# Low parts of split weights by a copy on ScalarE and an accumulating DMA, in a hybrid encoder block on one Trainium2 core

## The chip, the cores and the metric

The kernel runs on one core of one Trainium2 chip. The core has five engines that work at the same time, each through its own list of instructions and strictly in that list's order: TensorE (PE in the profile; its weight loads are shown apart, as PEld), VectorE (DVE), ScalarE (ACT), GpSimd (POOL) and SyncE (SP), which in this kernel only issues DMAs. Sixteen DMA engines move data between HBM and SBUF, and within SBUF. Engines wait for one another by semaphores. The metric is the device time of one execution in microseconds (us); less is better. The kernel before takes 2143.35 us, the median of three runs (2143.24 to 2143.78).

## The reference

One layer of an encoder on 1024 tokens of width 1024, in float32:

```python
h = rms_norm(x, g_mix)
glu_a, glu_b, q, k, v, z, a_in, b_in, gate_a, gate_b = split_cols(h @ w_in)
c = glu_a * sigmoid(glu_b)
c = silu(layer_norm(depthwise_conv(c, conv_dw_w) + conv_dw_b))       # 31 taps
y_conv = c @ w_conv_out
q, k, v = split_cols(silu(depthwise_conv([q, k, v], qkv_conv_w)))    # 5 taps
o = gated_delta_rule(q, k, v, ...) forward + the same backward       # 8 heads, chunks of 64
y_delta = (rms_norm(o) * silu(z)) @ w_delta_out
x = x + (sigmoid(gate_a) * y_conv + sigmoid(gate_b) * y_delta) @ w_o
gt, up = split_cols(rms_norm(x) @ w_gate_up)                         # 2 x 2816 columns
x = x + (silu(gt) * up) @ w_down
x = x + sigmoid(rms_norm(x) @ w_pl_gate) * rms_norm(p @ w_pl_proj)
return rms_norm(x, g_final)
```

Nearly all arithmetic is in the dense products with `w_in`, `w_conv_out`, `w_delta_out`, `w_o`, `w_gate_up`, `w_down` and `w_pl_gate`. All of them have the same form in the kernel, and the change is in how their weights are prepared.

## The kernel before, in words

**Split products.** TensorE reads the operands of a dense product as float32r, a form of float32 with fewer bits. To keep the precision, every operand is the sum of two such tiles, a high part `hi` and a low part `lo`, and a product is three matmuls (`mm3`): hi by hi, hi by lo of the activations, lo of the weights by hi. The first two need only `hi` of the weight tile; the third needs its `lo`. `split` makes the two parts from a float32 tile: ScalarE copies the tile into `hi`, which rounds it (`CAST` in the profile), and VectorE subtracts `hi` from the tile into `lo`.

**Weight tiles.** A weight tile is 512 rows by 128 columns, as four blocks of 128x128 side by side: 128 partitions by 512 values. SyncE loads it from HBM into a raw tile (four slots of tag `raw`, or one of the eight shared `mid` slots), `split` fills a tile of pool `wp` (tag `w`, `[P, 2, 4, P]`: both parts), and TensorE uses it as the stationary operand in 12 matmuls of 512 columns (four blocks, three matmuls each) or in 24, when both halves of the tokens follow one another. Pool `wp` has six slots (`N_W`), and tiles of a line are given out in the order of the program. `load_w` loads and splits; `split_w` splits a tile that is there already.

**Products of sums.** The delta projection (`seven`) and the gate and up products of the FFN (`gate_up`, `product`, `first_half`) use Winograd's form of Strassen's product: seven products in place of eight, of sums of the weights' quarters a11, a12, a21, a22. The sums are made by VectorE, some of them in place. In program order a block of `gate_up` uses the weights a11, s = a21 + a22, then s - a11 written over s, a11 - a21 written over a21, a12, then a12 - s written over a12, and a22. So two of the seven tiles are sources of a split, are overwritten by VectorE and are split again at once: s and a12. There are 22 column blocks: the first (`GU_PLAIN = 1`) is done by plain products, whose four weight tiles stay in their slots between the two halves of the tokens; of the next four (`GU_AHEAD = 4`) the products of a11 and a12 are done ahead, between those halves, while x is still being prepared; the other 17 go through whole.

**Stages.** In time: RMSNorm and transposes of x; the products with `w_in`, interleaved with the depthwise convolutions (336 instructions `big<-big,cw` on VectorE) and the delta rule of 8 heads, in chains of small matmuls with VectorE and ScalarE between them; LayerNorm and `w_conv_out`; then `w_delta_out` with the merge, `w_o`, the FFN, the per-layer embedding and the final norm. The delta rule and the convolutions end near 1100 us.

**What sets the order.** The block is written down as a list of instructions on stand-ins for tiles. `Plan.order` gives it an order by list scheduling: for each engine it takes, among the instructions whose inputs are there by its own clock, the most urgent one; durations, latencies and numbers of buffers are constants in the code (a 512-column float32r matmul is 512/2400 + 0.003 = 0.216 us in it). The order is fixed when the program is built; on the chip each engine only follows its list and waits. Weight splits have a more urgent level than the work they feed. Every operation is recorded by a helper, so one line of code stands for many instructions: L237 matmul, L242 transpose, L259 ScalarE copies and casts, L266 ScalarE activations, L282 VectorE, L310, L314 and L318 GpSimd (powers, memsets, selects), L330 SyncE's DMAs. In the profile, `w` is a weight tile, `raw` and `mid` its sources, `ps` a PSUM bank, `m` a tile of 512 columns in the delta rule's output step, `rn` its norm factors.

Of the kernel before, what the change touches and what calls it, by code (L numbers as in the profile page):

```python
# [36 lines left out]
class Buf:  # L37
    """A stand-in for a tile."""
# [15 lines left out]
class View:  # L54
    """Part of a tile: partitions [p0, p1), free dimensions as (stride, size) from an offset."""
# [40 lines left out]
    def fold(self, *sizes):  # L96
        """The last free dimension cut into dimensions of these sizes."""
        s, n = self.dims[-1]
        dims = []
        for k in reversed(sizes):  # L100
            dims.append((s, k))
            s *= k
        return View(self.buf, self.p0, self.p1, self.off, self.dims[:-1] + dims[::-1], self.cast)
# [4 lines left out]
    def spread(self, *shape):  # L108
        """Dimensions of size one repeated to these sizes."""
# [28 lines left out]
class Op:  # L138
    """An instruction: its engine, how to issue it, and what it reads and writes."""


# functions that need a table of their own in ScalarE, and the price of a change of tables
# [3 lines left out]
# a DMA: from its issue to its data, and bytes in a microsecond  # L146
DMA_LAT, DMA_RATE = 1.6, 300000.0
HOLD = {"dve": 0.24, "act": 0, "pe": 0}

# from the end of an instruction to the start of one that needs it, by the engines of both  # L150
# [7 lines left out]
class VPool:  # L158
# [5 lines left out]
    def tile(self, shape, dtype=F32, tag=None, bufs=None, line=None, cap=99, stream=None):  # L164
        """line: tiles of a line are given out in the order of the program, at most cap at a time."""
# [7 lines left out]
class Plan:  # L173
# [11 lines left out]
    # -- recording  # L185
    def add(self, eng, fn, outs, ins, cost, nbytes=0, table=None):
# [3 lines left out]
        o.idx = len(self.ops)  # L190
        o.key = (self.level, o.idx)
# [38 lines left out]
    # -- engines  # L230
    def matmul(self, out, lhsT, rhs, start, stop):
        n = rhs.n
        if rhs.buf.dtype == F32R and rhs.cast is None:
            cost = max(0.107, n / 2400 + 0.003)
        else:
            cost = 2 * max(0.107, n / 1200)
# [4 lines left out]
    def transpose(self, out, in_, ident):  # L241
        self.add("pe", lambda: self.nc.tensor.transpose(out.ap(), in_.ap(), ident.ap()), [out], [in_, ident], 0.107)  # L242
# [91 lines left out]
    # -- scheduling  # L334
    def order(self):
# [6 lines left out]
        free_slots = {}     # (pool, tag) -> times at which slots come free  # L342
        queue = {}          # line -> tiles in program order
# [8 lines left out]
        wait = {e: [] for e in engs}       # heap by ready time: dependencies all scheduled  # L352
        avail = {e: [] for e in engs}      # heap by key: ready at the engine's time
# [6 lines left out]
        held = []                            # of a later phase  # L360
        last_end = {}
        parked = {}                          # (pool, tag) -> ops that wait for a slot
# [10 lines left out]
        def slots_ready(o, now):  # L373
            """None when it can go now; else (time or None, (pool, tag))."""
# [20 lines left out]
        while len(done) < total:  # L395
# [43 lines left out]
            # worth the wait: something more urgent is about to be ready  # L439
# [24 lines left out]
            else:  # L464
                free[e] = o.end = now + o.cost
# [36 lines left out]
    # -- issue  # L502
# [54 lines left out]
# slots of each kind of tile, and what goes before what  # L557
# [11 lines left out]
YT_AFTER = (2, 1)  # L569
WO_LEAD = 6  # L570
# [9 lines left out]
# products of part 1 in order (k, q, v, g: glu, z, l: logits, p: per-layer embedding; with the head or  # L580
# block), and those that fill in
# [6 lines left out]
def ORDER(f):  # L588
    """The block up to the delta rule's end, in the order in which it is written down."""
# [1176 lines left out]
```

## Time and profile before

| | |
|---|---|
| runs before | 2143.78, 2143.35, 2143.24 us; median 2143.35 |
| span of the profiled execution | 2144.9 us, 1.5 us above the median of the runs |
| TensorE busy | 2094.7 us (98%), 10434 instructions |
| VectorE busy | 1606.4 us (75%) |
| ScalarE busy | 1089.8 us (51%) |
| GpSimd busy | 129.5 us (6%) |
| VectorE's low parts of weights, `w<-raw,w` and `w<-mid,w` | 340 + 125 instructions, 221.6 + 85.9 us |
| DMA | 278.69 MB, mean 130 GB/s |

How to read it. The profile is of one execution on the chip. Busy shares are averages over stages with different limits, so they are read by stage with the view that cuts the time into windows. The view of waits says for each engine how long it stood idle and what it waited for last. The chain is the work that ended last, followed back. A line of a group reads: line, engine, operation, output<-inputs by tile names, shapes, count | busy time, mean time of one in ns | idle time of the engine before it, and what ended it. A landing time of a DMA runs from its issue to its data.

### The profile page before, as it was taken

Reading aid. Unit: us, or ns where it says so; the run is one execution under the profiler, and the core shown is the slowest. Engines: PE = TensorE matmul, PEld = TensorE weight load, DVE = VectorE, ACT = ScalarE, POOL = GpSimd, SP = SyncE. Lnnn points to the kernel's source line nnn. Section 1 sums busy time; section 2 is a strip of 40 time slices with the busy share of each in tenths; the row PEclk is TensorE's granted clock in tenths of the full one; section 3 lists DMA queues with packets and bytes.
Section 4 is the critical chain, followed back from the end, with each engine's and each line's share of the span. In section 5 each row is a group of like instructions: output and inputs, shape, how many; then the busy total and the mean of one; then the engine's idle time right before and its main releaser. Section 6 shows DMA issues by size and latency. Waiting matters only on the chain.

```text
span 2144.9 us, 29696 instructions
## 1 busy us (share of the span) xinstructions
PE 2094.7 (98%) x10434; PEld 1736.6 (81%) x10434; DVE 1606.4 (75%) x2621; ACT 1089.8 (51%) x2501; POOL 129.5 (6%) x203
## 2 busy tenths in 40 slices
PE   7999999999999999999999999999999999999998
PEld 5888788878888788878888888888888888888888
DVE  4488999977898989887687868786666667452676
ACT  6636656756656655767775435533323334121542
POOL 1000201110100111011100000000000000000000
PEclk9999999999999999999999999999999999999999
DMA  6233224522423422635468687432222227231253
GB/s 213 100 123 127 84 81 138 187 79 79 138 89 120 146 74 79 197 122 182 157 213 254 195 262 229 123 99 84 80 78 84 84 80 273 67 95 39 66 170 108
DMA packets 289077, 278.69 MB, mean 130 GB/s; under 512 B 17209, under 2 KB 217074, under 8 KB 288928
## 3 DMA queue, kind: packets, MB, share of 16 engines
q1 hardware_dynamic: 288928, 276.79, 40.3%
q8 instruction: 82, 1.34, 0.3%
q14 instruction: 67, 0.55, 0.1%
HBM read 198.02 MB, written 78.71 MB: 129 GB/s over the span
## 4 chain that ended last, share of the span: by engine, by line
PE 86%; ACT 7%; DVE 5%; issue 1%; DMA 1%; SPq 0%; POOL 0%; DVEq 0%; POOLq 0%; ACTq 0%
PE ps L237 84%; ACT big L259 4%; DVE big L282 3%; PE ps L242 2%; DVE mid L282 1%; ACT big L266 1%; ACT m L266 1%; DVE w L282 1%; ACT w L259 1%; DMA big<-in_x_dram 1%; DMA d<-mid 0%; ACT mid L266 0%; SPq L330 0%; ACT L266 0%; ACT mid L259 0%
## 5 line engine op out<-in xcount | busy, mean ns | idle before, releaser
L237 PE MATMUL ps<-big,w 128*128 128x512 f32 (+1 forms) x7524 | 1848.7, 399 | 0.9 <-ACT w L259 0.8
L237 PEld LDWEIGHTS ps<-big,w 128*128 128x128 f32 x7524 | 1383.4, 189 | 305.3 <-ACT w L259 1.2
L282 DVE SCALAR_TENSOR_TENSOR big<-big,cw 128x1024 f32<-128x1024 f32 x336 | 434.2, 1299 | 17.3 <-ACT big L266 12.3
L259 ACT CAST w<-raw 128x512 fp32r<-128x512 f32 (+2 forms) x340 | 198.3, 589 | 365.0 <-PE ps L237 288.4
L282 DVE TENSOR_TENSOR w<-raw,w 128x512 fp32r<-128x512 f32 (+2 forms) x340 | 221.6, 659 | 124.9 <-ACT w L259 119.3
L282 DVE TENSOR_TENSOR big<-ps,big 128x512 f32<-128x512 f32 (+1 forms) x132 | 89.9, 687 | 86.4 <-PE ps L237 76.2
L259 ACT CAST w<-mid 128x512 fp32r<-128x512 f32 x125 | 77.2, 621 | 149.5 <-PE ps L237 109.5
L282 DVE TENSOR_TENSOR w<-mid,w 128x512 fp32r<-128x512 f32 x125 | 85.9, 688 | 62.3 <-ACT w L259 61.6
L237 PEld LDWEIGHTS ps<-big 128*128 128x128 f32 x784 | 101.9, 195 | 16.1 <-issue 9.1
L237 PE MATMUL ps<-big 128*128 128x128 f32 (+1 forms) x784 | 107.2, 283 | 7.7 <-ACT big L259 5.1
L282 DVE TENSOR_TENSOR big<-big 128x512 fp32r<-128x512 f32 (+2 forms) x159 | 107.0, 707 | 8.7 <-ACT big L259 8.4
L259 ACT COPY big<-big 32x128 f32<-32x128 f32 (+1 forms) x264 | 102.5, 440 | 16.5 <-DVE big L282 12.5
L259 ACT COPY big<-ps 32x128 f32<-32x128 f32 (+3 forms) x162 | 66.8, 413 | 64.3 <-PE ps L237 55.0
L259 ACT CAST big<-big 128x512 fp32r<-128x512 f32 x120 | 69.9, 619 | 42.5 <-DVE big L282 21.3
L242 PE MATMUL ps<-ident,big 128*128 128x128 f32 (+1 forms) x432 | 72.0, 280 | 13.6 <-DMA big<-in_x_dram 9.3
L237 PEld LDWEIGHTS ps<-S,big 128*128 128x128 f32 x448 | 71.8, 190 | 10.0 <-DVE S L282 0.2
L237 PE MATMUL ps<-S,big 128*128 128x128 f32 x448 | 75.0, 275 | 0.0
L242 PEld LDWEIGHTS ps<-ident,big 128*128 128x128 f32 (+1 forms) x432 | 53.9, 147 | 25.2 <-issue 13.4
L237 PEld LDWEIGHTS ps<-big,m 128*128 128x128 f32 x512 | 64.1, 195 | 12.2 <-ACT m L266 9.4
L237 PE MATMUL ps<-big,m 128*128 128x128 f32 x512 | 66.1, 280 | 6.4 <-ACT m L266 6.3
L266 ACT ACTIVATE mid<-mid 128x512 f32<-128x512 f32 (+2 forms) x87 | 50.2, 580 | 38.6 <-DVE mid L282 26.8
L266 ACT ACTIVATE big<-big 128x1024 f32<-128x1024 f32 (+2 forms) x80 | 56.6, 715 | 22.2 <-DVE big L282 17.2
(158 smaller groups left out, 1711.0 us busy)
## 6 DMA issues: line engine op xcount, KB each, us to landing
d<-mid SPq DMA_DIRECT2D x162, 256.0 KB, 3.0
raw<-in_w_in_dram SPq DMA_DIRECT2D x128, 256.0 KB, 3.0
mid<-d SPq DMA_DIRECT2D x120, 256.0 KB, 3.4
big<-d SPq DMA_DIRECT2D x92, 256.0 KB, 4.0
big<-dqkv SPq DMA_DIRECT2D x32, 512.0 KB, 4.9
raw<-in_w_gate_up_dram SPq DMA_DIRECT2D x50, 256.0 KB, 2.9
dqkv<-big SPq DMA_DIRECT2D x24, 512.0 KB, 2.9
mid<-in_w_gate_up_dram SPq DMA_DIRECT2D x46, 256.0 KB, 4.0
```

The source lines that it names most:

```text
L237: o = self.add("pe", lambda: self.nc.tensor.matmul(out.ap(), lhsT.ap(), rhs.ap(), start=start, stop=stop), [out], [lhsT, rhs], cost)
L242: self.add("pe", lambda: self.nc.tensor.transpose(out.ap(), in_.ap(), ident.ap()), [out], [in_, ident], 0.107)
L259: return self.nc.scalar.copy(out.ap(), in_.ap())
L266: return self.nc.scalar.activation(out.ap(), in_.ap(), func, **kw)
L282: return getattr(e, name)(**{k: v.ap() if isinstance(v, View) else v for k, v in kw.items()})
```

## The change

Three things change, and all other text of the kernel stays (line numbers rise by 3 to 17).

1. A new helper `split_dma` takes the place of `split` in `load_w` and `split_w`, that is for the 465 weight tiles. ScalarE writes `hi` as before, then writes `lo` as the tile times -1, rounded in the same way, which is -hi; then GpSimd issues a DMA within SBUF that adds the raw tile to `lo` (`accum_op=ALU.add`). VectorE's subtraction is gone. The low part is now the unrounded difference as the DMA leaves it. Activations are still split by `split`, with VectorE.
2. The planner learns of the new operation (1.2 us on GpSimd, the data 3.0 us after that) and gets other prices for matmuls: 512/2208 + 0.0015 = 0.233 us for 512 columns in place of 0.216, and 0.111 and 0.110 in place of 0.107 for the shortest ones. Since the order comes from these prices, all lists of instructions are new.
3. The 16 loads of the residual x in `resid` wait for another store of the merge, `d_yt[5][1]` in place of `d_yt[2][1]` (`RE_AFTER`).

```diff
+ADD_ISSUE, ADD_TAIL = 1.2, 3.0
...
         o.idx = len(self.ops)
+        o.tail = 0.0
...
         if rhs.buf.dtype == F32R and rhs.cast is None:
-            cost = max(0.107, n / 2400 + 0.003)
+            cost = max(0.111, n / 2208 + 0.0015)
         else:
-            cost = 2 * max(0.107, n / 1200)
+            cost = 2 * max(0.111, n / 1200)
...
+    def dma_add(self, out, in_):
+
+        o = self.add("pool", lambda: self.nc.gpsimd.dma_start(out=out.ap(), in_=in_.ap(), accum_op=ALU.add),
+                     [out], [in_, out], ADD_ISSUE)
+        o.tail = ADD_TAIL
...
-                free[e] = o.end = now + o.cost
+                free[e] = now + o.cost
+                o.end = free[e] + o.tail
...
+RE_AFTER = (5, 1)
...
+    def split_dma(hi, lo, src):
+
+        pn.act(hi, src)
+        pn.act(lo, src, scale=-1.0)
+        pn.dma_add(lo.f(), src)
+
     def load_w(w, r0, nk, c0, cap=4, pool=None):
...
-            split(t[:, 0, :n], t[:, 1, :n], raw[:, :n])
+            split_dma(t[:, 0, :n], t[:, 1, :n], raw[:, :n])
...
     def split_w(src):
         t = wp.tile([P, 2, HK, P], F32R, tag="w", line="w", cap=N_W, stream="rest")
-        split(t[:, 0], t[:, 1], src)
+        split_dma(t[:, 0], t[:, 1], src)
...
-        pn.dma(e, d_xT[b][h], also=[d_yt[YT_AFTER[0]][YT_AFTER[1]]])
+        pn.dma(e, d_xT[b][h], also=[d_yt[RE_AFTER[0]][RE_AFTER[1]]])
```

Below are three places where the lists differ. A row is line, instruction, output<-inputs, shape; what stands in brackets at its end are the queues whose semaphores it waits for (DMASW are DMAs issued by GpSimd, DMAHW those issued by SyncE, PE, DVE and Activation the engines).

**VectorE, the output step of one head pair's delta rule** (`rn` are the norm factors, computed by GpSimd from the second row here; `m` the normed outputs that TensorE transposes next). Before:

```order
L282 TENSOR_TENSOR rn<-rn,sso 128x8
L282 TENSOR_SCALAR rn<-rn 128x8
L282 SCALAR_TENSOR_TENSOR big<-big,cw_606 128x1024
L282 TENSOR_TENSOR w<-raw,w 128x512
L282 TENSOR_TENSOR m_5886<-big,rn 128x512
L282 TENSOR_TENSOR w<-raw,w 128x512
L282 TENSOR_TENSOR m_5904<-big,rn 128x512
```

The same step now:

```order
L285 TENSOR_TENSOR rn<-rn,sso 128x8
L285 TENSOR_SCALAR rn<-rn 128x8
L285 SCALAR_TENSOR_TENSOR big<-big,cw_522 128x1024
L285 SCALAR_TENSOR_TENSOR big<-big,cw_620 128x1024
L285 TENSOR_TENSOR m_5844<-big,rn 128x512
L285 TENSOR_TENSOR m_5848<-big,rn 128x512
```

The two low parts of weights that stood between `rn` and the two `m` are gone; one tap of a convolution stands there instead.

**TensorE, the products of a11 and a12 that are done ahead**, when four of the six weight slots hold the tiles of the plain block (`w_13129` and `w_13147`, now `w_13364` and `w_13388`, are the weights of one column block). Before:

```order
L237 MATMUL ps_13143<-big_12731,w_13129 128x512 [waits Activation_49]
L237 MATMUL ps_13143<-big_12731,w_13129 128x512
L237 MATMUL ps_13143<-big_12731,w_13129 128x512 [waits DVE_49]
L237 MATMUL ps_13143<-big_12743,w_13129 128x512 x3
...
L237 MATMUL ps_13168<-big_12793,w_13147 128x512 [waits Activation_49]
L237 MATMUL ps_13168<-big_12793,w_13147 128x512
L237 MATMUL ps_13168<-big_12793,w_13147 128x512 [waits DVE_49]
```

Now:

```order
L240 MATMUL ps_13381<-big_12903,w_13364 128x512 [waits Activation_49]
L240 MATMUL ps_13381<-big_12903,w_13364 128x512
L240 MATMUL ps_13393<-big_12958,w_13388 128x512 [waits Activation_49]
L240 MATMUL ps_13393<-big_12958,w_13388 128x512
L240 MATMUL ps_13381<-big_12903,w_13364 128x512 [waits DMASW2_49]
L240 MATMUL ps_13381<-big_12913,w_13364 128x512 x3
...
L240 MATMUL ps_13393<-big_12958,w_13388 128x512 [waits DMASW3_49]
```

The third matmul of a tile now waits for a DMA of GpSimd, and the two matmuls of the next tile that need only `hi` stand ahead of it. The column block after this one has the same pattern; the last of the four has ten matmuls of the plain block in addition between the first two of its second tile and the third of its first.

**VectorE, one block of `gate_up`** (`mid_14474` and `mid_14965` are s of a block, `mid_14456` and `mid_14944` its a12; `ps` banks are finished products). Before:

```order
L282 TENSOR_TENSOR w_14629<-mid_14474,w_14629 128x512 [waits Activation_49]
L282 TENSOR_TENSOR mid_14474<-mid_14474,raw_14354 128x512 [waits DVE_49]
L282 TENSOR_TENSOR w_14648<-mid_14474,w_14648 128x512 [waits Activation_49]
...
L282 TENSOR_TENSOR w_14688<-mid_14456,w_14688 128x512 [waits DMAHW3_49,Activation_49]
L282 TENSOR_TENSOR m2_14588<-ps_14662,m2_14588 128x512 [waits DVE_49]
L282 TENSOR_TENSOR mid_14456<-mid_14456,mid_14474 128x512 [waits DVE_49]
```

Now:

```order
L285 TENSOR_TENSOR m2_15036<-ps_15108,m2_15036 128x512 [waits DVE_49,PE_49]
L285 TENSOR_TENSOR mid_14965<-mid_14965,raw_14851 128x512 [waits DMASW6_49,Activation_49]
L285 TENSOR_TENSOR mid_15137<-mid_15137,m2_15036 128x512 [waits Activation_49]
L285 TENSOR_TENSOR mid_15132<-ps_15113,mid_15132 128x512 [waits PE_49]
L285 TENSOR_TENSOR mid_15132<-mid_15132,lnb_15110 128x512 [waits DVE_49]
L285 TENSOR_TENSOR mid_14944<-mid_14944,mid_14965 128x512 [waits DMAHW1_49,DMASW1_49,Activation_49]
```

s - a11 and a12 - s, which overwrite a tile that was just split, waited for VectorE's own subtraction before; now they wait for the DMA that reads this tile, and the first of them stands behind the evacuation of the previous block's product `ps_15108`.

More of the change, by code (lines that the diff above doesn't have):

```diff
@@ L138 @@
 class Op:
+    pass
 TABLES = {AF.Exp: 0, AF.Sigmoid: 1, AF.Silu: 2, AF.Ln: 3}
@@ L241, in transpose @@
     def transpose(self, out, in_, ident):
-        self.add("pe", lambda: self.nc.tensor.transpose(out.ap(), in_.ap(), ident.ap()), [out], [in_, ident], 0.107)
+        self.add("pe", lambda: self.nc.tensor.transpose(out.ap(), in_.ap(), ident.ap()), [out], [in_, ident], 0.110)
     def act(self, out, in_, func=AF.Copy, scale=1.0, bias=None, accum=None):
```

## The prediction

> **What bounds the kernel now.** The page first: busy shares, the slices of TensorE, the chain that ended last.
>
> ```profile
> span 2144.9 us, 29696 instructions
> PE 2094.7 (98%) x10434; PEld 1736.6 (81%) x10434; DVE 1606.4 (75%) x2621; ACT 1089.8 (51%) x2501; POOL 129.5 (6%) x203
> ...
> PE   7999999999999999999999999999999999999998
> ...
> PE 86%; ACT 7%; DVE 5%; issue 1%; DMA 1%; SPq 0%; POOL 0%; DVEq 0%; POOLq 0%; ACTq 0%
> ```
>
> TensorE is busy nearly throughout, and the chain is 86% TensorE. Since a busy TensorE can still be slowed, windows by stage (columns: window, its length, then PE, PEld, DVE, ACT, POOL busy, granted clock, DMA share, GB/s):
>
> ```profile
> 0.00:1100.00 1100.00, 1059.51 (x5740) 891.41 (x5741) 893.90 (x1448) 700.38 (x1820) 120.26 (x191) 0.99 0.39 127
> 1100.00:2080.00 980.00, 980.00 (x4240) 790.94 (x4239) 666.42 (x1066) 368.79 (x628) 4.03 (x4) 1.00 0.43 134
> 2080.00:2145.00 65.00, 55.16 (x458) 54.23 (x456) 46.09 (x109) 20.65 (x55) 5.26 (x8) 0.95 0.37 118
> 1020.00:1040.00 20.00, 15.83 (x93) 14.33 (x94) 8.93 (x17) 13.34 (x34) 3.15 (x2) 0.83 0.40 127
> 1500.00:1600.00 100.00, 100.00 (x430) 80.53 (x429) 66.00 (x102) 30.77 (x51) 0.00 (x0) 1.00 0.26 79
> ```
>
> From 1100 to 2080 us TensorE never stops: 430 matmuls of 512 columns in 100 us, 0.2326 us each, 2.79 us for a weight tile used 12 times. In these 980 us nothing can be gained, only lost. All there is to gain lies in the first 1100 us: 40.5 us idle, and a granted clock of 0.99, which drops where TensorE waits (0.83 in the fourth row). TensorE's own waits from 100 to 1100 us:
>
> ```profile
> PE ps L242 <- DVE m L282: 11.2, 5, 3.7
> ...
> PE ps L237 <- ACT m L266: 6.3, 5, 2.4
> PE ps L237 <- ACT big L259: 5.1, 3, 3.3
> ...
> PE ps L237 <- DVE big L282: 1.4, 2, 1.0
> ...
> PE ps L237 <- issue: 1.1, 1, 1.1
> ...
> PE ps L237 <- ACT w L259: 0.8, 1, 0.8
> ```
>
> Together 25.9 us. Freeing VectorE, at 81% here, is worth at most what stands behind it in this list, not the 307 us that its subtractions take.
>
> **The change part by part.** *Removed: 465 subtractions on VectorE.* Their price is where they hold something up. Two of the waits for `m`, in order of time:
>
> ```profile
> 551.61 2.59 POOL L310 TENSOR_TENSOR rn<-rn,mhalf 128x8 f32<-128x8 f32 x1 [8.98 <-DVE rn L282]
> 555.76 0.69 DVE L282 TENSOR_TENSOR w<-raw,w 128x512 fp32r<-128x512 f32 x1 [1.73 <-ACT w L259]
> 556.37 1.29 DVE L282 TENSOR_TENSOR m<-big,rn 128x512 f32<-128x512 f32 x2
> 557.11 0.77 PE L242 MATMUL ps<-ident,m 128*128 128x128 f32 x4 [3.21 <-DVE m L282]
> 787.53 1.64 POOL L310 TENSOR_TENSOR rn<-rn,mhalf 128x8 f32<-128x8 f32 x1 [8.07 <-DVE rn L282]
> 790.10 0.69 DVE L282 TENSOR_TENSOR w<-raw,w 128x512 fp32r<-128x512 f32 x1 [2.66 <-ACT w L259]
> 790.71 1.29 DVE L282 TENSOR_TENSOR m<-big,rn 128x512 f32<-128x512 f32 x2
> 791.45 0.66 PE L242 MATMUL ps<-ident,m 128*128 128x128 f32 x4 [3.71 <-DVE m L282]
> ```
>
> `rn` is there at 554.20 and 789.17, but VectorE's list has the low part of a weight next, which waits for a busy ScalarE; `m` starts only at 556.37 and 790.71. Without it, `m` starts some 2.0 and 1.5 us earlier: **-3.5 us**. The first pair of lists in the part on the change shows the obstacle gone.
>
> *Moved: the whole order.* The planner's matmul took 0.216 us, 7% less than the 0.2326 measured, now 0.233. With the true price, work is listed closer to where its inputs are really ready. Of the other 25.9 - 3.5 = 22.4 us of waits this can save anything from none to all; I take a third, since most of them are chains of latency, which no order shortens: **-7.5 us**. The lost clock is 1% of 1100 us, 11 us; idle time falls by 11 of 40.5 us, so about a quarter of it comes back: **-2.5 us** (0 to -11).
>
> *Added on ScalarE: a second pass over each tile.* Durations and counts:
>
> ```profile
> L259 ACT CAST w<-mid 128x512 fp32r<-128x512 f32 x125 | 77.2, 621 | 149.5 <-PE ps L237 109.5
> L282 DVE TENSOR_TENSOR w<-mid,w 128x512 fp32r<-128x512 f32 x125 | 85.9, 688 | 62.3 <-ACT w L259 61.6
> ...
> 0.00:1100.00 1100.00, 855.89 (x3214) 583.19 (x3215) 98.48 (x143) 86.68 (x144) 0.99 0.39 127
> 1100.00:1320.00 220.00, 218.71 (x936) 175.66 (x935) 52.95 (x80) 46.53 (x79) 1.00 0.77 246
> ```
>
> (The last two rows are windows of the weight tiles alone: PE, PEld, DVE, ACT.) A pass takes 0.62 us, a subtraction took 0.69. In the first 1100 us 144 more passes raise ScalarE from 64 to 72%. TensorE's 11.4 us of waits for ScalarE's `m` and `big` grow with that by an eighth, 1.4 us; a norm factor that now queues behind adds on GpSimd adds a little: **+2 us** (0 to +11.4, a doubling).
>
> *Added: 465 accumulating DMAs.* Call L the time from the end of the second pass to the sum in SBUF. The trace has no such DMA. Rows for a bound (issues: count, KB, us to landing; then GpSimd's dearest operation on a tile of this size):
>
> ```profile
> raw<-in_w_gate_up_dram SPq DMA_DIRECT2D x50, 256.0 KB, 2.9
> ...
> big<-dqkv SPq DMA_DIRECT2D x32, 512.0 KB, 4.9
> dqkv<-big SPq DMA_DIRECT2D x24, 512.0 KB, 2.9
> d<-big SPq DMA_DIRECT2D x32, 256.0 KB, 2.1
> raw<-in_w_delta_out_dram SPq DMA_DIRECT2D x8, 256.0 KB, 4.2
> ...
> L318 POOL TENSOR_SCALAR_AFFINE_SELECT m<-m 128x512 f32<-128x512 f32 x32 | 35.5, 1111 | 156.7 <-DMA m<-d 85.5 <-PE ps L237 31.7 <-ACT z L266 29.3
> ```
>
> Least: 2.1, a store of 256 KB, its issue included. Most: 4.9 for 512 KB into SBUF, the add's two inputs, and 1.1 on GpSimd, 6.0. I take a load of 256 KB in the FFN's stage, 2.9, plus 0.8 for the second input (2.9 less 2.1 from `big`), plus 0.7 by which GpSimd may issue later than SyncE: **L = 4.4 us**. A low part then comes 1.24 + 4.4 = 5.6 us after its source, not 1.3. In the Trainium skill, "DMA: Bandwidth & Descriptors", section "Anatomy of one DMA — SWDGE (gpsimd) path", fits a DMA issued by GpSimd by 2.0 us plus its bytes at 436 GB/s, an estimate of 2.6 us here. No run here shows it; with it the sum below would come to 2133.
>
> Mostly this is covered. At the start, weights are split about 15 us before use:
>
> ```profile
> 4.74 0.62 ACT L259 CAST w<-raw 128x512 fp32r<-128x512 f32 x1 [0.27 <-DMA raw<-in_w_in_dram]
> ...
> 19.64 0.39 PE L237 MATMUL ps<-big,w 128*128 128x512 f32 x1
> ```
>
> Where all six slots of weights rotate, a slot is free five tiles, 14 us, before its next tile is needed. The residual's 16 loads, moved later, hide behind the six half-blocks of `w_o` that go ahead, 6 x 2.79 us. Cover is gone at three places.
>
> First, the products done ahead. Two slots rotate; from a slot's last matmul, two passes and L must pass, while TensorE has ten matmuls of the other tile and two and two of the next: 14 x 0.2326 = 3.26 us. Each pair stalls 1.24 + L - 3.26 = L - 2.0. The lists show two pairs of this form and a fourth with ten more matmuls (2.33 us): 2 x 2.4 + 0.1 = **+5 us** (0.2 at L = 2.1; 9.7 at 6.0).
>
> Second, the 17 whole blocks of `gate_up`. Overwriting s and a12 must now wait until an add has read them, so two adds follow one another in each block, and everything behind them in order waits too. Followed from the landing of one block's last sum (a12 - s) to the next block's: ten matmuls of that product 2.33, its evacuation and s - a11 on VectorE 1.38, six passes (three tiles) 3.72, L, a12 - s 0.69, three passes 1.86, L: 9.98 + 2L. A block's 84 matmuls take 19.54 us. At L = 4.4 the loop takes 18.8 and is hidden by TensorE: **0**. It becomes the path at **L = 4.8**; at 6.0 it costs 17 x 2.4 = 41 us. This is the term that decides.
>
> Third, the four blocks of `w_delta_out` have the same loop. Loads land 4.2 us after issue there, not 2.9; L = 5.7 makes 21.4 us, 4 x 1.8 = 7.4, most of which the 14 us of lead from the stage before takes up: **+2 us** (0 to +14).
>
> Sum: -3.5 - 7.5 - 2.5 + 2 + 5 + 0 + 2 = -4.5 us, a span of 2140.4 against 2144.9. The profiled execution is 1.5 us above the runs' median; the same difference there gives 2143.35 - 4.5, about **2139 us**.
>
> **The rivals.**
>
> *The loop of adds is the bound* (slower). L is 5.4 in `gate_up`: 17 x 1.24 = +21 us, ahead +8, delta projection +8, first part -11.5: 2169 us. For it: one DMA of 512 KB into SBUF took 4.9. Against: DMA share is only 0.26 in this stage. It decides from 4.8 us, 0.4 above my value.
>
> *The DMA engines are the bound* from 1100 to 1320 us, at a share of 0.77 already.
>
> ```profile
> 1780.00:1800.00 20.00, 20.00 (x88) 16.06 (x87) 19.10 (x34) 13.76 (x28) 0.00 (x0) 1.00 1.06 382
> ```
>
> The busiest stretch reaches 1.06 at 382 GB/s, so 256 KB take 0.73 us of all engines. With 80 adds, one such price each lifts 0.77 to 1.04, double to 1.30, 53 us too much; it decides from 0.8 us an add. With the residual's loads deferred (12 us) and half the rest elastic, +20: 2159 us. The same page, section "Issuing engines are not separate DMA queues", says that a DMA from GpSimd shares these 16 engines; by that rule the adds compete here, and the trace can only show how full the engines are (0.77).
>
> *ScalarE becomes the bound of the first part*: its waits double (+11.4), the reordering saves nothing: -3.5 + 11.4 + 5 + 2 = +15, 2158 us. For it: copies on ScalarE already hold up the delta rule (5.1 us). Against: 28% stays idle.
>
> *Most of the waits dissolve and adds are quick*, L = 3.0: -3.5, -16, clock -5, ahead +2: 2121 us.
>
> **How the numbers follow.** Chances: forecast 0.52, loop 0.22, DMA engines 0.07, ScalarE 0.06, dissolving waits 0.13. The forecast's own range is 2127 to 2148: -16 where two thirds of the waits go, +4.5 where none go and 1 us of the clock comes back (-3.5 - 1 + 2 + 5 + 2). Over 0.2% (4.3 us, what a measurement here can tell from no change) means below 2139.1 or above 2147.6. The forecast sits at the first of these; its 0.52 split 0.29 faster, 0.20 the same, 0.03 slower. Faster: 0.29 + 0.13 = 0.42; the same 0.20; slower: 0.03 + 0.22 + 0.07 + 0.06 = 0.38. The ends of all bounds are 2107 and 2216; leaving out a tenth on each side, 2121 to 2180.
>
> **What would show it.** In the profile after: VectorE at 72% before 1100 us and no wait of TensorE for `m` behind a weight; TensorE waiting for `w` in two or three stalls of 2 to 3 us around 1340 to 1390 us, a sign of the products ahead; between 1400 and 1760 us 430 matmuls per 100 us still, or about 405 if the loop decides; DMA share below 1 from 1100 to 1320 us. L is read from the adds' landing times: above 4.8 us the forecast is wrong, and it is also wrong if TensorE's waits before 1100 us exceed 26 us.

## The result, and the profile after

The changed kernel takes 2338.65 us, the median of four runs (2332.74 to 2339.78), against 2143.3 us (2142.39 to 2143.78): a ratio of 1.0911, 95% interval 1.0895 to 1.0926. It is 195 us slower, far outside the predicted range of 2121 to 2180 us. First the page of the kernel after: busy shares, the DMA engines in 40 slices, the two DMA queues (packets, MB, share of 16 engines), and the chain.

```profile
span 2338.1 us, 31301 instructions
PE 2166.1 (93%) x10434; PEld 1766.5 (76%) x10434; DVE 1328.5 (57%) x2146; ACT 1306.7 (56%) x2973; POOL 540.6 (23%) x678
...
DMA  7466344743474436466699899868777879754594
...
q1 hardware_dynamic: 288928, 276.79, 37.0%
q0 software_dynamic: 68400, 118.26, 30.1%
...
PE 30%; DMA 17%; issue 9%; ACT 4%; DVE 3%; POOL 1%; SPq 0%; POOLq 0%; DVEq 0%; ACTq 0%
```

VectorE lost 278 us of work, as the change says (1606.4 to 1328.5). TensorE's busy time rose by 71 us at the same 10434 instructions, and its idle time from 50 to 172 us (span less busy): 71 + 122 is the whole difference of the spans, 193 us. The chain was 86% TensorE and is now 30%, with DMA at 17%. A new queue, the adds that GpSimd issues, takes 30.1% of all 16 DMA engines.

By stage, the kernel before (window, length, then PE, PEld, DVE, ACT, POOL busy, granted clock, DMA share, GB/s; its first 1100 us are in the prediction):

```profile
1100.00:1300.00 200.00, 200.00 (x858) 161.12 (x857) 154.00 (x248) 104.12 (x173) 0.00 (x0) 1.00 0.75 239
1300.00:1600.00 300.00, 300.00 (x1303) 242.42 (x1302) 220.43 (x350) 111.05 (x186) 2.01 (x2) 1.00 0.36 112
1600.00:1900.00 300.00, 300.00 (x1286) 241.52 (x1286) 187.56 (x300) 91.97 (x161) 0.00 (x0) 1.00 0.35 114
```

and after:

```profile
0.00:1100.00 1100.00, 1019.45 (x5434) 848.62 (x5435) 784.17 (x1265) 739.33 (x1896) 226.59 (x318) 0.97 0.54 148
1100.00:1300.00 200.00, 180.69 (x747) 141.89 (x747) 84.94 (x138) 106.31 (x198) 45.65 (x50) 0.93 0.89 230
1300.00:1600.00 300.00, 258.76 (x1037) 201.56 (x1036) 137.91 (x217) 145.79 (x263) 74.35 (x86) 0.93 0.89 219
1600.00:1900.00 300.00, 296.57 (x1261) 235.85 (x1260) 127.23 (x196) 135.41 (x248) 89.71 (x103) 1.00 0.78 169
```

The first 1100 us lose 40 us (idle 40.5 to 80.6). The worst stretch is 1100 to 1600 us, in which nothing was to be lost: TensorE stands idle for 60 us, at a granted clock of 0.93, and does 1784 matmuls in place of 2161. The DMA share there is 0.89, and up to 1.05 in single windows of 100 us. From 1600 to 1900 us, in the middle of `gate_up`, 3.4 us are idle: the loop of adds is hidden there. TensorE's longest waits after:

```profile
PE ps L240 <- DMA w<-raw: 42.0, 29, 4.2
PE ps L240 <- DMA w<-mid: 33.5, 25, 4.0
PE ps L240 <- ACT big L262: 20.9, 5, 7.6
PE ps L245 <- DVE m L285: 13.4, 4, 4.1
```

The first two kinds did not exist before: a weight's low part that has not landed. Landing times from the view of DMA issues, after:

```profile
w<-raw POOLq DMA_DIRECT2D x300, 256.0 KB, 4.5
...
mid<-d SPq DMA_DIRECT2D x120, 256.0 KB, 5.0
...
raw<-in_w_conv_out_dram SPq DMA_DIRECT2D x32, 256.0 KB, 5.0
raw<-in_w_o_dram SPq DMA_DIRECT2D x32, 256.0 KB, 4.4
```

and the same loads before:

```profile
mid<-d SPq DMA_DIRECT2D x120, 256.0 KB, 3.4
...
raw<-in_w_conv_out_dram SPq DMA_DIRECT2D x32, 256.0 KB, 4.1
raw<-in_w_o_dram SPq DMA_DIRECT2D x32, 256.0 KB, 3.8
```

The adds' own landing (minimum, median, maximum) from the group of GpSimd's DMA line, in the windows 100 to 500, 1100 to 1600 and 1600 to 1900 us of the kernel after:

```profile
DMA to landing us min/median/max: 3.2/3.6/7.8
...
DMA to landing us min/median/max: 3.3/5.1/8.8
...
DMA to landing us min/median/max: 3.3/4.4/6.5
```

So an add takes 3.2 us at best and 4.4 us in `gate_up`, but 5.1 us where the DMA share is 0.89, and loads, also those of spilled tiles (`d`), take longer beside it. Not all of that is the adds': in the first experiment below, which has none, `mid<-d` takes 3.9 us, a load of `w_conv_out` 4.7 and one of `w_o` 4.5. The Trainium skill, "DMA: Bandwidth & Descriptors", section "Anatomy of one DMA — SWDGE (gpsimd) path", has the fit from which the prediction took an estimate of 2.6 us; the fastest 256 KB adds took 3.2 us here, so for a DMA that adds the trace decides against it.

### The profile page after: what moved, and what is told of

Same layout as the page of the kernel before. It is cut to its first block, busy times and chain, and to the rows that moved or that the text cites. A ratio compares the mean times of both kernels' runs of the same rounds, so it can differ in the third digit from the quotient of the medians.

```text
span 2338.1 us, 31301 instructions
## 1 busy us (share of the span) xinstructions
PE 2166.1 (93%) x10434; PEld 1766.5 (76%) x10434; DVE 1328.5 (57%) x2146; ACT 1306.7 (56%) x2973; POOL 540.6 (23%) x678
## 3 DMA queue, kind: packets, MB, share of 16 engines
q0 software_dynamic: 68400, 118.26, 30.1%
## 4 chain that ended last, share of the span: by engine, by line
PE 30%; DMA 17%; issue 9%; ACT 4%; DVE 3%; POOL 1%; SPq 0%; POOLq 0%; DVEq 0%; ACTq 0%
PE ps L240 30%; DMA w<-mid 7%; DMA w<-raw 4%; DMA raw<-in_w_conv_out_dram 2%; DMA raw<-in_w_o_dram 1%; DVE big L285 1%; DVE mid L285 1%; ACT big L262 1%; DMA raw<-in_w_pl_gate_dram 1%; POOL w L339 1%; ACT w L269 1%; DMA big<-d 1%; ACT mid L269 1%; DMA mid<-d 0%; PE ps L245 0%
## 5 line engine op out<-in xcount | busy, mean ns | idle before, releaser
L240 PE MATMUL ps<-big,w 128*128 128x512 f32 (+1 forms) x7524 | 1895.4, 405 | 88.9 <-DMA w<-raw 42.0
L240 PEld LDWEIGHTS ps<-big,w 128*128 128x128 f32 x7524 | 1403.9, 192 | 425.8 <-DMA w<-raw 56.6
L339 POOL DMA_DIRECT2D w<-raw x340 | 303.3, 906 | 1188.4 <-ACT w L269 763.9
L269 ACT ACTIVATE w<-raw 128x512 fp32r<-128x512 f32 (+2 forms) x340 | 202.7, 599 | 0.1
L339 POOL DMA_DIRECT2D w<-mid x125 | 118.9, 1003 | 358.0 <-ACT w L269 211.3
L285 DVE TENSOR_TENSOR mid<-mid 128x512 f32<-128x512 f32 (+3 forms) x68 | 41.6, 612 | 168.7 <-DMA w<-mid 117.6
L240 PE MATMUL ps<-big 128*128 128x128 f32 (+1 forms) x784 | 115.4, 298 | 18.3 <-ACT big L262 13.0
L240 PEld LDWEIGHTS ps<-big 128*128 128x128 f32 x784 | 108.3, 208 | 28.9 <-issue 11.5
L285 DVE TENSOR_TENSOR mid<-ps,mid 128x512 f32<-128x512 f32 x66 | 45.3, 686 | 72.9 <-PE ps L240 41.8
L285 DVE STREAM_TRANSPOSE big<-big 32x128 f32<-32x128 f32 (+2 forms) x56 | 43.3, 778 | 76.0 <-ACT big L262 60.5
```

What stands on the lines that cost most here:

```text
L240: o = self.add("pe", lambda: self.nc.tensor.matmul(out.ap(), lhsT.ap(), rhs.ap(), start=start, stop=stop), [out], [lhsT, rhs], cost)
L269: return self.nc.scalar.activation(out.ap(), in_.ap(), func, **kw)
L285: return getattr(e, name)(**{k: v.ap() if isinstance(v, View) else v for k, v in kw.items()})
L339: o = self.add("pool", lambda: self.nc.gpsimd.dma_start(out=out.ap(), in_=in_.ap(), accum_op=ALU.add), [out], [in_, out], ADD_ISSUE)
```

## The experiments

Times are medians of four runs; the kernel before, run beside them, took 2141.84 to 2143.76 us.

**The order alone.** VectorE's subtraction is put back in both places, so that the new prices and the later loads of the residual are left:

```diff
-            split_dma(t[:, 0, :n], t[:, 1, :n], raw[:, :n])
+            split(t[:, 0, :n], t[:, 1, :n], raw[:, :n])
...
-        split_dma(t[:, 0], t[:, 1], src)
+        split(t[:, 0], t[:, 1], src)
```

> The changed kernel with VectorE's subtraction put back in both places: what is left of the change are the new matmul prices and the later loads of the residual, and so a new order. My prediction's term for the order (-7.5 and -2.5 us of clock) gives about 2133 us, 2125 to 2145. The rival, that the new order itself costs part of the 195 us (it was made with the adds in view): over 2150 us.

Measured: 2185.7 us, ratio 1.0203 (1.0188 to 1.0219). The rival is right: without a single add, the new order costs 43 us. (These lists are planned for the subtraction, so they are not the changed kernel's lists less the adds; the 43 us and the 153 above them are differences of whole kernels.) Which of its two edits does it? The kernel before with the prices alone:

```diff
-            cost = max(0.107, n / 2400 + 0.003)
+            cost = max(0.111, n / 2208 + 0.0015)
...
-            cost = 2 * max(0.107, n / 1200)
+            cost = 2 * max(0.111, n / 1200)
...
-        self.add("pe", lambda: self.nc.tensor.transpose(out.ap(), in_.ap(), ident.ap()), [out], [in_, ident], 0.107)
+        self.add("pe", lambda: self.nc.tensor.transpose(out.ap(), in_.ap(), ident.ap()), [out], [in_, ident], 0.110)
```

> The kernel before with the new matmul prices alone (0.233 us in place of 0.216), subtraction on VectorE, the residual's loads as before. The new order with both edits cost +42 us. If the prices do it (a planner that holds TensorE for slower than before leaves loads and splits later, with less to spare): 2175 to 2195 us. If the later loads of the residual do it: 2140 to 2155 us.

Measured: 2186.37 us, 1.0196 (1.0180 to 1.0213). It is the prices, all of it; the residual's later loads change nothing that can be measured. TensorE's waits in this kernel, of the kinds that the prediction wanted to shorten:

```profile
PE ps L242 <- DVE m L282: 18.4, 6, 4.7
PE ps L237 <- ACT big L259: 13.4, 4, 4.3
```

They were 11.2 us for `m` and 5.1 us for `big`; the order with the true price lengthens them. Of the 41 us between the profiled spans (2185.7 and 2144.9 us), 26 are TensorE's idle time, which rises from 50 to 76 us, and 15 are longer matmuls (2094.7 to 2109.7 us busy). Which placements in the new lists do it stays open.

**A ladder of prices.** Only the price of a 512-column matmul is changed, to 512/X + 0.003 with X = 2738, 2560, 2306.3 and 2115.7:

```diff
-            cost = max(0.107, n / 2400 + 0.003)
+            cost = max(0.107, n / 2738.0 + 0.003)
```

> The kernel before with one number changed: the planner's price of a 512-column matmul is 0.190 us (it was 0.216; 0.2326 is measured; 0.233 gave 2186 us). Theory M (margin: a planner that holds TensorE for quicker than it is puts the work of the other engines further ahead of their use, and a true price takes that lead away): lower is no worse, 2130 to 2150 us, and the series 0.190, 0.203, 0.225, 0.245 rises with the price. Theory T (tuning: the other constants of the order were found for 0.216, and any other price spoils it): 2160 to 2200 us, on both sides of 0.216.

> As above with 0.203 us. Theory M: 2135 to 2148 us. Theory T: 2155 to 2190 us.

> As above with 0.225 us, halfway to the new price. Theory M: between the two ends, 2155 to 2175 us. Theory T: anything from 2155 to 2190 us, with no order in the series.

> As above with 0.245 us, more than the measured 0.2326. Theory M: worse than at 0.233, 2190 to 2215 us. Theory T: 2155 to 2200 us, not tied to the price.

Measured, with the two prices already known:

| price in the planner, us | median, us | ratio (95%) |
|---|---|---|
| 0.190 | 2245.49 | 1.0475 (1.0448 to 1.0502) |
| 0.203 | 2194.61 | 1.0226 (1.0201 to 1.0252) |
| 0.216 (before) | 2143 | 1 |
| 0.225 | 2167.42 | 1.0106 (1.0080 to 1.0131) |
| 0.233 (with the change's prices for short ones) | 2186.37 | 1.0196 (1.0180 to 1.0213) |
| 0.245 | 2186.28 | 1.0196 (1.0176 to 1.0216) |

The margin theory, which wanted the lower prices to be no worse, has fallen. Both sides rise from 0.216, as the tuning theory said, though with some order in the series; it did not foresee how much 0.190 costs, and 0.203 ends 5 us above its range. A price next to the measured 0.2326 is no better than one that is 7% off. That the other constants (levels, caps, leads) were found together with 0.216 fits this; no run changes them.

**The two places of the adds.** Subtraction put back in `load_w` alone (the first pair of lines of the first diff), so that the adds of `split_w` stay. These are 179 and not 125, as the expectation has it: 125 is the number with a source named `mid`, and 54 more in this run have a `raw` tile as their source.

> The changed kernel with VectorE's subtraction put back in load_w alone: 125 adds stay, for the sums of weights' quarters in the delta projection and in gate_up, 340 go. Raw slots of load_w are free early again. Theory A: what is left are the products ahead and the delta projection, +7 to +25 us on the new order: 2140 to 2170 us. Theory B (traffic): the adds between 1260 and 1600 us are 40 of 131, so a third of that stretch's loss stays, and little else: 2165 to 2190 us.

Measured: 2238.59 us, 1.0452 (1.0432 to 1.0472), 53 us above the order alone and above both expectations. Neither had the order's 43 us; with it the nearer one would have ended at 2233. Subtraction put back in `split_w` alone (the second pair), so that the other 296 adds stay (there are 475 in all: 465 into tiles named `w`, and 10 into tiles of another pool, for `w_pl_gate`):

> The changed kernel with VectorE's subtraction put back in split_w alone: 340 adds stay, for the tiles that load_w brings, 125 go. The counterpart (adds in split_w alone) took 53 us more than the order without adds (2186 us). If the two parts simply add up, this one takes 2338 - 53 = about 2285 us (2275 to 2295). If they share a full resource (DMA engines from 1100 to 1600 us), less than the sum: 2240 to 2275 us.

Measured: 2286.02 us, 1.0661 (1.0644 to 1.0678): 100 us above the order alone. The parts add up: 43 + 53 + 100 = 196. With only the 179 adds of `split_w` one sees where those of the sums cost something. Windows of that kernel: the delta projection, the products ahead, the whole blocks of `gate_up`, and its end:

```profile
1260.00:1330.00 70.00, 55.81 (x206) 41.97 (x205) 36.55 (x58) 27.04 (x49) 11.88 (x14) 0.88 0.85 227
...
1440.00:1500.00 60.00, 54.47 (x222) 42.69 (x223) 34.41 (x54) 31.97 (x59) 15.78 (x19) 0.97 0.68 148
1500.00:1830.00 330.00, 328.21 (x1397) 261.33 (x1397) 145.82 (x223) 150.31 (x275) 99.37 (x114) 1.00 0.80 173
1830.00:1920.00 90.00, 80.51 (x332) 62.72 (x331) 53.86 (x90) 39.10 (x75) 10.52 (x12) 0.98 0.78 228
```

and the adds' landing in the first (here from 1240 to 1345 us), third and fourth of these stretches:

```profile
DMA to landing us min/median/max: 3.3/6.2/9.3
...
DMA to landing us min/median/max: 3.3/4.4/5.8
...
DMA to landing us min/median/max: 3.3/6.4/9.2
```

The first of these stretches again, with the order alone and with the thin adds of an experiment below, and the landing of the thin adds in it:

```profile
1260.00:1330.00 70.00, 70.00 (x301) 56.43 (x300) 55.04 (x88) 33.35 (x58) 0.00 (x0) 1.00 0.85 273
...
1260.00:1330.00 70.00, 58.88 (x227) 44.66 (x226) 34.27 (x55) 34.09 (x63) 17.42 (x20) 0.93 0.72 207
...
DMA to landing us min/median/max: 2.2/3.8/4.9
```

A stretch of 70 us holds 301 matmuls of 0.2326 us, and the order alone does them; with the adds of the sums the delta projection does 206. The products ahead do 222 of 258, 8 us lost, of which 4.4 are two waits for an add. In the whole blocks 1.8 of 330 us are idle. That is the loop of adds which the prediction followed: at 4.4 us it is hidden, and at the end of `gate_up`, where an add takes 6.4 us, TensorE waits again. In the delta projection the landing time alone does not decide it: thin adds land there after 3.8 us, and TensorE still does only 227 matmuls.

**The traffic, without the delay.** The kernel before, its lists unchanged; GpSimd stores both parts of each full weight tile to HBM, which nobody reads:

```diff
+    def store(t, n):
+        if n == 4:
+            scr = dp.tile([P, 2, 4, P], F32R, tag="scr", bufs=16)
+            pn.add("pool", lambda: pn.nc.gpsimd.dma_start(out=scr.ap(), in_=t.ap()), [scr], [t], 0.0)
...
             split(t[:, 0, :n], t[:, 1, :n], raw[:, :n])
+            store(t, n)
...
         split(t[:, 0], t[:, 1], src)
+        store(t, 4)
```

> The kernel before, all other lists unchanged, with one extra DMA for each full weight tile: GpSimd stores both parts of the tile (512 KB) to HBM once the low part is there. Nobody waits for these stores but the slot's next tile. They bring the DMA engines about the work of the adds (two times 0.73 us of all engines by the busiest stretch of before; an add took 1.5) without holding a raw tile and without delaying a low part. Theory A (raw slots): 2145 to 2170 us, TensorE hardly waits. Theory B (full DMA engines slow all loads and spills): at least half of the 195 us, 2240 us or more, with the loss between 1100 and 1500 us.

Measured: 2222.65 us, 1.0375 (1.0360 to 1.0391): 81 us, between the two. The queue, the stores and two groups of loads, and two windows:

```profile
q0 software_dynamic: 62640, 228.09, 28.9%
...
scr<-w POOLq DMA_DIRECT2D x425, 512.0 KB, 4.7
...
raw<-in_w_conv_out_dram SPq DMA_DIRECT2D x32, 256.0 KB, 7.2
raw<-in_w_o_dram SPq DMA_DIRECT2D x32, 256.0 KB, 8.9
```

```profile
1100.00:1300.00 200.00, 182.47 (x748) 141.72 (x748) 134.49 (x214) 89.24 (x145) 31.34 (x59) 0.97 1.02 345
1300.00:1600.00 300.00, 277.62 (x1167) 221.72 (x1166) 204.52 (x327) 109.90 (x187) 52.68 (x97) 0.95 0.89 295
```

The stores take 28.9% of the engines, nearly the adds' 30.1%, and loads of `w_o` land after 8.9 us in place of 3.8. Every low part is made by VectorE as before, and yet TensorE stands idle for 40 us between 1100 and 1600 us, with the DMA engines at 1.02 and 0.89. (A store also holds its weight slot until it has landed, and it writes to HBM, which an add within SBUF does not; how much of the 81 us is due to either, this run does not tell.) In the Trainium skill, "DMA: Bandwidth & Descriptors", section "Issuing engines are not separate DMA queues", DMAs of GpSimd share the 16 engines with those of SyncE; by that rule the loads must suffer, and the 8.9 us agree.

**The delay, without the traffic.** The changed kernel, each add cut to an eighth of its tile:

```diff
-        o = self.add("pool", lambda: self.nc.gpsimd.dma_start(out=out.ap(), in_=in_.ap(), accum_op=ALU.add),
+        def part(v):
+            return View(v.buf, v.p0, v.p1, v.off, [(1, v.n // 8)], v.cast)
+
+        o = self.add("pool", lambda: self.nc.gpsimd.dma_start(out=part(out).ap(), in_=part(in_).ap(), accum_op=ALU.add),
```

> The changed kernel, each add cut to the first eighth of its tile (128 partitions x 64 values, 32 KB in place of 256 KB); the rest of the low part stays -hi, so part of the sum is left out. Lists, waits and the number of adds are the same; their traffic falls from 30% of the DMA engines' time to about 4%, and an add's landing from 4.4 us to perhaps 3. The order alone (all subtractions back on VectorE) costs 42 us, 2186 us, and the adds 153 us on top. Theory B (traffic of the adds on the full DMA engines): nearly all of the 153 us goes, 2190 to 2215 us. Theory C (the round of an add: weight slots and raw slots are held for its landing time, whatever it moves): the landing falls by a third, so some 50 of the 153 us go: 2270 to 2300 us. Both at once: between.

Measured: 2239.29 us, 1.0444 (1.0424 to 1.0464). It lies between the two theories: of the 153 us that the adds cost, 99 go with their bytes and 53 stay. The same rows as above:

```profile
q0 software_dynamic: 68400, 14.81, 8.2%
...
w<-raw POOLq DMA_DIRECT2D x300, 32.0 KB, 2.7
...
raw<-in_w_conv_out_dram SPq DMA_DIRECT2D x32, 256.0 KB, 3.9
raw<-in_w_o_dram SPq DMA_DIRECT2D x32, 256.0 KB, 3.8
```

```profile
1100.00:1300.00 200.00, 183.81 (x756) 144.13 (x755) 85.33 (x132) 114.13 (x202) 49.87 (x58) 0.97 0.73 204
1300.00:1600.00 300.00, 290.95 (x1242) 231.51 (x1241) 156.03 (x244) 163.12 (x292) 87.36 (x101) 0.99 0.58 152
```

Loads are back at 3.8 to 3.9 us, and the clock at 0.97 and 0.99. The cut also shortens the landing from 4.5 to 2.7 us, so the 99 us are bytes and the wait for them together.

The 53 us also hold the second pass on ScalarE and GpSimd's issues, which no run takes out alone. The trace says how much that can be. TensorE is idle for 109 us, 39 more than with the order alone. Its waits that end with an add's landing are 32.3 us, where those for VectorE's low parts were 4.8; all its waits for ScalarE rise from 24.1 to 31.6 us. So most of the added idle time ends with a landing.

**The raw slots.** In `load_w` the add takes its second input from HBM, so that the raw slot is free after ScalarE's second pass:

```diff
...
+                     self.nc.gpsimd.dma_start(out=out.ap().bitcast(F32R), in_=real.bitcast(F32R), accum_op=ALU.add),
...
-        pn.dma_add(lo.f(), src)
+        pn.dma_add(lo.f(), src, real)
...
-            split_dma(t[:, 0, :n], t[:, 1, :n], raw[:, :n])
+            split_dma(t[:, 0, :n], t[:, 1, :n], raw[:, :n], rows_.rearrange("(k q) c -> q k c", q=P))
```

> The changed kernel with one edit: in load_w the add takes its second input from the weights in HBM, not from the raw tile in SBUF. All five engines keep their lists, the add keeps its size and its wait, but a raw slot is free after the second ScalarE pass (about 1.3 us after its load) and not only when the add has landed (4.5 to 5 us more). Theory A (the four raw slots go round too slowly): in the profile of the change a raw slot is reloaded only after its add, a round of about 12 us for load, passes and add, or 3 us a tile and more where only two slots are used, against 2.79 us of matmuls a tile. Freed, a round is about 7 us, 1.8 us a tile; the stretch from 1100 to 1600 us gives back 60 to 90 us and the first 1100 us some 20: 2220 to 2265 us. Theory B (the DMA engines are full: a share of 1.0 from 1200 to 1500 us, 1.5 us of all engines for an add): the engines move as much as before, nothing comes back: 2315 to 2350 us. Theory C (the length of the add itself, between the low part's two steps, is what TensorE waits for): 2300 to 2340 us, since the add takes as long.

Measured: 2378.06 us, 1.1099 (1.1081 to 1.1118), slower than any theory had it. The run did not do what it was made for:

```profile
q0 software_dynamic: 169776, 118.26, 36.1%
...
w<-in_w_conv_out_dram POOLq DMA_DIRECT2D x32, 256.0 KB, 7.4
raw<-in_w_o_dram SPq DMA_DIRECT2D x32, 256.0 KB, 7.9
w<-in_w_o_dram POOLq DMA_DIRECT2D x32, 256.0 KB, 8.2
```

An add from HBM lands after 7.4 to 8.2 us and takes more of the engines, so the slot's gain can't be told from the add's loss. Hence the same with thin adds:

```diff
...
+                     self.nc.gpsimd.dma_start(out=part(out).ap().bitcast(F32R),
+                                              in_=real[:, :part(out).n].bitcast(F32R), accum_op=ALU.add),
...
-            split_dma(t[:, 0, :n], t[:, 1, :n], raw[:, :n])
+            split_dma(t[:, 0, :n], t[:, 1, :n], raw[:, :n], rows_[:P])
```

> The changed kernel with thin adds, and in load_w their second input comes from HBM, so that a raw slot is free right after the second ScalarE pass. Against the thin adds from SBUF (2239 us) only the hold of the raw slots changes, with little traffic this time. If the raw slots' round is part of the remaining 53 us: 2200 to 2225 us. If it is the weight tile that comes late: 2230 to 2250 us.

Measured: 2234.6 us, 1.0429 (1.0404 to 1.0454), against 2239.29 with the slots held: 5 us, or 0.2%. This time the slots are free earlier: SyncE's waits for an add that reads a raw tile fall from 769 to 180 us. The landing stays the same where most is lost, 3.9 and 4.2 us for `w_conv_out` and `w_o` against 4.0 and 4.1 from 1100 to 1420 us; with `w_in` it is 2.9 in place of 2.3, which can hide a little. The raw slots are not the main part of the 53 us.

**The adds on the old order.** The lists of before, with the cast doubled on ScalarE, VectorE's row left empty and GpSimd's add in its place; the planner still plans a subtraction:

```diff
+    def split_add(hi, lo, src):
+        def both():
+            pn.nc.scalar.copy(hi.ap(), src.ap())
+            pn.nc.scalar.activation(lo.ap(), src.ap(), AF.Copy, scale=-1.0)
+
+        split(hi, lo, src)
+        pn.ops[-2].fn = both
+        pn.ops[-1].fn = lambda: pn.nc.gpsimd.dma_start(out=lo.f().ap(), in_=src.ap(), accum_op=ALU.add)
...
-            split(t[:, 0, :n], t[:, 1, :n], raw[:, :n])
+            split_add(t[:, 0, :n], t[:, 1, :n], raw[:, :n])
...
-        split(t[:, 0], t[:, 1], src)
+        split_add(t[:, 0], t[:, 1], src)
```

> The kernel before with its own order kept, and only the subtraction replaced: wherever ScalarE's list has the cast it now has the cast and the negated pass, and where VectorE's list had the subtraction there is nothing, and GpSimd issues the add. The planner knows nothing of it. If the loss is the sum of an order away from the tuned one (43 us) and of the adds (153 us): 2143 + 153 = about 2296 us (2280 to 2310). If an order that plans the add's landing hides part of it: more than 2320 us (the changed kernel took 2339, with old prices 2327).

Measured: 2424.67 us, 1.1311 (1.1291 to 1.1332): 281 us, not 153. With thin adds:

> The same with each add cut to an eighth of its tile (the rest of the low part stays -hi). On the new order the thin adds cost 53 us over VectorE's subtraction. If that is the add's own delay (2.5 to 2.7 us from issue to landing, with slots held for it): 2143 + 53 = about 2196 us (2180 to 2215). If it is the list made for the adds and not the adds: 2143 to 2165 us.

Measured: 2250.78 us, 1.0505 (1.0480 to 1.0531): 107 us, more than either expectation. So an add costs time without its bytes too, and not through the new list, and planning it helps: the changed kernel with the old prices, whose planner knows of the adds, as expected and measured (the short prices go back in the same way):

```diff
-            cost = max(0.111, n / 2208 + 0.0015)
+            cost = max(0.107, n / 2400 + 0.003)
```

> The changed kernel with the old, too low matmul prices, so with the order's larger margins, and the adds. If the new prices' 42 us and the adds' 153 us add up: about 2296 us. If margins in the order are what hides the adds' landing: less, 2230 to 2280 us. If the adds fill the DMA engines, whatever the order: 2290 to 2340 us.

Measured: 2326.78 us, 1.0851 (1.0824 to 1.0879), 98 us better than the unplanned adds at the same prices, and 12 us better than the change. The prices' 43 us and the adds' 153 are not independent of the order: on the old prices planned adds cost 184 us.

No version that keeps any of the adds, and no other price, is as fast as the kernel before.

## Why the prediction was wrong

The sum was -4.5 us; measured is +195. On the new order the difference divides into 43 us (prices), 53 us (thin adds) and 99 us (the rest of the bytes, with the longer landing that they bring).

- **"Moved: the whole order ... -7.5 us", and the clock's -2.5.** The step that failed is "With the true price, work is listed closer to where its inputs are really ready." It came out at +43 us. The bound "anything from none to all" of the waits had no place for a loss: I took waits as a stock to be saved, while a new list makes its own. It needed a range on both sides, since every list is made anew when one price moves.

- **"Added: 465 accumulating DMAs", the price on the DMA engines.** I took 0.73 us of all 16 engines for 256 KB and put the case that they fill up among the rivals, with 0.07 and 20 us. An add takes 30.1% of 2338.1 us over 118.26 MB, or 451 tiles: 1.56 us, twice as much, and "it decides from 0.8 us an add" was my own threshold. The rival was right in kind, and its "double" would have been the price; but it was worked out for 1100 to 1320 us alone, and it excused half with elasticity. The full stretch reaches to 1600 us, the traffic also slows spills, loads and adds elsewhere, and with the longer landing it costs 99 us.

- **"L = 4.4 us."** The median landing is 4.5 and 4.4 us from the add's issue on GpSimd, and in one case followed in the trace the issue came 0.3 us after the second pass. So the sum was close, though the 0.7 in it for a later issue had no row behind it. As one number for all stages it failed: it is 5.1 in the median from 1100 to 1600 us and 6.2 in the delta projection. L depends on the traffic that the adds themselves bring, and the sum had them as separate terms.

- **"Mostly this is covered."** The six slots' lead of 14 us was to hide everything in `load_w`, at 0 us. Its 296 adds cost 100 us. The thin adds still cost 53 over both places, and TensorE waits for `w<-raw` in the first 1100 us too. I first blamed the raw tiles, which are now held until the add has read them; 5 us is all that freeing them gave. Which part of the 53 us is the low part coming late, and which the weight slots that are bound meanwhile, stays open: the runs don't separate them.

- **The loop of `gate_up`, "0", deciding at L = 4.8.** Right. In the whole blocks 4.4 us from issue to landing, 4.7 with the 0.3 ahead of it, leave TensorE at 328.2 of 330 us busy; that is 0.1 us below the deciding value, so partly luck. The products ahead were right too: two waits of 4.4 us together, where I had +5. The delta projection was not: the stretch loses 22 us by its matmuls, where I had +2 and at most 14. The loop gives only 4 x 2.8 = 11 us at the 6.2 us measured there, and with thin adds, at 3.8 us, it would be hidden, yet 17 us are lost. TensorE's waits there still end with an add's landing (9.1 us for `w<-mid` with thin adds), so either the loop is longer than I priced it or another chain of adds binds; which of them stays open.

- **"Added on ScalarE", +2.** Right beside the order alone: TensorE's waits for ScalarE's `m` and `big` from 100 to 1100 us are 15.5 us with it and 15.8 after. The rise from 11.4 to 15.5 is the order's.

- **"Without it, `m` starts some 2.0 and 1.5 us earlier."** The obstacle is gone, the wait is not. In time order, VectorE, GpSimd and TensorE after:

```profile
569.77 0.17 DVE L285 TENSOR_SCALAR rn<-rn 128x8 f32<-128x8 f32 x1
569.86 2.60 DVE L285 SCALAR_TENSOR_TENSOR big<-big,cw 128x1024 f32<-128x1024 f32 x2
570.03 2.63 POOL L313 TENSOR_TENSOR rn<-rn,mhalf 128x8 f32<-128x8 f32 x1 [8.98 <-DVE rn L285]
...
572.69 1.29 DVE L285 TENSOR_TENSOR m<-big,rn 128x512 f32<-128x512 f32 x2 [0.24 <-POOL rn L313]
...
573.44 0.66 PE L245 MATMUL ps<-ident,m 128*128 128x128 f32 x4 [3.42 <-DVE m L285]
```

  `m` now starts 0.03 us after GpSimd's `rn`, with no weight between, and TensorE waits 3.42 us all the same, for the chain of norm factors. Its waits for `m` are 13.4 us in 4 pieces where they were 11.2 in 5. What the subtraction's place was worth is seen where the order is held. On the lists of before, the waits for `m` fall from 11.2 us to 7.4 with the thin adds and 4.3 with whole ones (other waits have grown there, so part of it may be theirs); with the new prices they fall from 17.9 (order alone) to 13.4. So -3.5 was of the right size, and the new order had added more before.

- **The clock.** I had it gain. It went down where TensorE waits: 0.93 from 1300 to 1600 us, where a matmul takes 258.76/1037 = 0.250 us against 300/1303 = 0.230 before. Of the 193 us of the spans, 71 are such longer matmuls.

## What to carry to other kernels

An accumulating DMA is not free because the compute engines are: price it in time of the DMA engines, which was here twice that of a plain transfer, and set that beside the DMA share of each stage before asking what it hides behind. VectorE at 81% with few waits behind it had little to sell; look at what ends TensorE's waits, not at how busy the engine beside it is. And test a new price in a list scheduler apart from the change that it comes with: the more accurate number was 43 us slower, and no reading of the waits foretold it.

## What was unexpected of the hardware

The prices of DMAs that GpSimd issues, as time of all 16 engines (share times span, over the number of tiles, counted as full ones by their bytes): a plain store to HBM, for each 256 KB, 0.289 x 2219.1 / 870 = 0.74 us; an add within SBUF 1.56 us; an add of 32 KB 0.082 x 2235.1 / 451 = 0.41 us, a quarter of the whole add's time for an eighth of its bytes; an add from HBM about 2.1 us, an estimate (36.1% of 2379.2 us, less the 179 adds of `split_w` within SBUF at 1.56, over the other 272 full tiles). The thin add still lands only after 2.7 us in the median, and after 4.0 between 1100 and 1230 us.
